# A FoX and RWKV-7 layer: weight sums of seven-part products made ahead, during the input projections, and kept in memory; eight sets a pair instead of six

## The chip, the core and the metric

The kernel runs on one core of a Trainium2 chip. The metric is the device time of one launch in microseconds (us). Matrix products run on TensorE (PE; its weight loads are PEld), two-input vector work on VectorE (DVE), casts and activations on ScalarE (ACT), some element-wise work on GpSimd (POOL). SyncE (SP) issues nearly all DMA transfers.

## What is computed

One layer on 256 rows of width 4096: an input projection, two groups of heads, an output projection, a layer norm. The attention and the recurrence are left out here; they run beside the projections in both kernels.

```python
proj = jnp.einsum('bsd,dc->bsc', x, w_in)           # 256 x 4096 by 4096 x about 16,600
...
h = jnp.concatenate([fox_out, rwkv_out], axis=-1) * jax.nn.silu(z.astype(f32))
out = jnp.einsum('bsc,cd->bsd', h.astype(x.dtype), w_out)   # 256 x 4096 by 4096 x 4096
x = _layernorm(ALPHA * x.astype(f32) + out.astype(f32), ln_gain, ln_bias, LN_EPS).astype(x.dtype)
```

All of it is float32. PE multiplies a rounded type (fp32r) faster than float32, so each operand is cut into a rounded part `hi` and the rest `lo`, and a product is three matmuls: hi by hi, lo by hi, hi by lo.

## The kernel before

**Jobs.** The weights come in jobs of two k-rows of 128 by 512 columns: 128x1024 float32, 512 KB. `load` (L268) has SP fetch one into one of four raw buffers (tag "wr"). `split` makes `hi` by a cast on ACT (L151, four buffers) and `lo` by a subtraction on DVE (L152, three buffers). `fetch` and `weights` keep three jobs made ahead of the one that PE works on; up to three more are loaded or loading. In the input projections a job has 12 matmuls (L157, L158, L159): two k-rows, two halves of 128 rows, three matmuls each. There are 8 groups n of 4 column blocks b of 16 jobs, the first block apart.

**Sides.** The gates, the recurrence (`chain`), the attention and the moving of results are Python generators, each advanced one step at every `slot()`, two slots a job. So their instructions stand between those of the projections, at places that counted waits (`wait(n)`) choose. Each engine takes its instructions in the order in which they were written.

**Output projection.** `plan` lists the jobs of 8 blocks of 512 columns. Blocks 0, 1, 2 and 7 are plain (kind "n"): four `product` calls of three matmuls (L994, L995, L997), so 12 matmuls. Blocks 3 and 4, and 5 and 6, form pairs. For the q in `FEW`, two k-rows of both blocks of a pair are one 2x2 product of blocks, done in a seven-part scheme (Winograd's form of Strassen's): seven products, 21 matmuls, in place of eight products, 24. They are four jobs: e1 (two products with the weights of block b as they are), e2 (one product, half a job of block b+1), e3 and e4 (two products each with sums of weights). The partial results p1, p5, p6, p7 have banks of their own and are added into the output by `merge` when the pair's last set is done. `FEW = range(6, 12)`: six sets a pair, twelve in all.

**Sums.** The left factors (sums of quarters of h) are made by GpSimd in `combine_left` and cut into hi and lo in `split_left`, which writes `sq` and overwrites half of `ht[2q]`; six DMAs restore that half before block 7. The weight sums are made by GpSimd in `combine` (kinds t12: L309, L310; t34: L312, L313), four 128x512 subtractions a set, in the output projection, right before the jobs that use them. To have more raw weights in memory at once, the sets of every second q use places of their own (L259 in tag "lr", L265 in columns of `res`). `drain` runs deferred work (the merges, the residual) at points of the plan.

Of the kernel before, what the change touches and what calls it, by code (L numbers as in the profile page):

```python
# [17 lines left out]
P = 128  # L18
# [72 lines left out]
def layer(ctx: ExitStack, tc: tile.TileContext, xt, xtok, w_main, w_lora, w_first, muv, w_o, up, par, mulora, fbias, lng, lnb, cst, out):  # L91
# [128 lines left out]
    plan += [("n", 2, q) for q in sorted(range(KT // 2), key=lambda q: q not in FEW)]  # L220
    own_place = set()
    for b in (3, 5):
        plain = [[(n, q) for q in range(KT // 2) if q not in FEW] for n in (b, b + 1)]
        units = []
        for q in FEW:
            units.append([plain[j].pop(LEAD if not j else 0) for j in range(2)])
        lead = plain[0]
        assert len(lead) == LEAD
        plan += [("n", *t) for t in lead[: LEAD - 2]]
        for n, q in enumerate(FEW):  # L230
            if n % 2 == 0:
                own_place.add((b, q))
            before = units[n - 1][1] if n else lead[-1]
            plan += [] if n else [("n", *lead[-2])]
            plan += [("t12", b, q), ("n", *before)] + ([("e4", b, FEW[n - 1])] if n else [])
            plan += [("t34", b, q), ("e1", b, q), ("n", *units[n][0]), ("e2", b, q), ("e3", b, q)]
        plan += [("n", *units[-1][1]), ("e4", b, FEW[-1])]
        plan += [("n", *t) for t in plain[1]]
    plan += [("n", NB - 1, q) for q in range(KT // 2)]
    loads = []  # L240
    for kind, b, q in plan:
        loads += [(b, q)] if kind == "n" else [(b, q), (b + 1, q)] if kind == "t12" else []
    stream += [(f"wo{b}_{q}", w_o[b][:, 2 * q : 2 * q + 2, :]) for b, q in loads]
# [7 lines left out]
    sums_of = {}  # L251

    def load():
        name, src = stream.pop()
        b, q = [int(t) for t in name[2:].split("_")] if name[:2] == "wo" else (0, 0)
        if b in PAIRS and (PAIRS[b], q) in own_place:
            if b == PAIRS[b]:
                raw = const.tile([P, 1024], F32, tag="lr", name=name)
                nc.sync.dma_start(out=raw, in_=src.rearrange("p k c -> p (k c)"))  # L259
                apart[name] = [raw[:, j * OB : (j + 1) * OB] for j in range(2)]  # L260
                apart[name, 0] = raw
            else:
                apart[name] = [res[j][:, (NB - 1) * OB :] for j in range(2)]
                for j in range(2):
                    nc.sync.dma_start(out=apart[name][j], in_=src[:, j, :])  # L265
            return
        raw = wpool.tile([P, 1024], F32, tag="wr", name=name, bufs=4)
        nc.sync.dma_start(out=raw, in_=src.rearrange("p k c -> p (k c)"))  # L268
        raws[name] = raw

    def fetch():
        while len(raws) < 3 and stream:
            load()
        job = jobs.pop()
        if job[0][0] in "et":
            combine(*job)
            return
        name = job[0] if len(job) == 1 else f"wo{job[1]}_{job[2]}"
# [12 lines left out]

    apart = {}

    def halves_of(name):
        while name not in raws and name not in apart:
            load()
        if name in apart:
            return apart[name]
        return [raws[name][:, j * OB : (j + 1) * OB] for j in range(2)]

    def combine(kind, b, q):
        one, two = f"wo{b}_{q}", f"wo{b + 1}_{q}"
        if kind in ("t12", "t34", "e2"):
            (b11, b21), (b12, b22) = (halves_of(t) if t == two or kind != "e2" else (None, None) for t in (one, two))
        g = nc.gpsimd.tensor_tensor
        if kind[0] == "t":
            t = sums_of[b, q, kind] = rpool.tile([P, 2 * OB], F32, tag="t", name=f"{kind}_{b}_{q}", bufs=2)
            if kind == "t12":
                g(t[:, :OB], b12, b11, ALU.subtract)  # L309
                g(t[:, OB:], b22, t[:, :OB], ALU.subtract)  # L310
            else:
                g(t[:, :OB], b22, b12, ALU.subtract)  # L312
                g(t[:, OB:], b21, sums_of[b, q, "t12"][:, OB:], ALU.subtract)  # L313
            return
        if kind == "e1":
            t, n = apart.get((one, 0)), 2 * OB
            t = raws.pop(one) if t is None else t
        elif kind == "e2":
            t, n = b22, OB
            raws.pop(two, None)  # L320
        else:
            t, n = sums_of[b, q, "t12" if kind == "e3" else "t34"], 2 * OB
        ready.append(((kind, b, q), *split(t, n, f"{kind}_{b}_{q}")))
# [557 lines left out]

    def chain():
        for n in range(G // 2):
            yield from rwkv(n)
# [131 lines left out]
    def combine_left(q):  # L1016
        e, o = ht[2 * q], ht[2 * q + 1]
        t = lefts[q] = rpool.tile([P, 2 * OB], F32, tag="t", name=f"sf{q}", bufs=2)
        he, ho = t[:, :S], t[:, S : 2 * S]
        s1, s2, s3, s4 = (t[:, 2 * S + n * P : 2 * S + (n + 1) * P] for n in range(4))  # L1020
        g = nc.gpsimd.tensor_tensor
        g(he, e[:, 0, :].bitcast(F32), e[:, 1, :].bitcast(F32), ALU.add)
        g(ho, o[:, 0, :].bitcast(F32), o[:, 1, :].bitcast(F32), ALU.add)
        g(s1, he[:, P:], ho[:, P:], ALU.add)
        g(s2, s1, he[:, :P], ALU.subtract)
        g(s3, he[:, :P], he[:, P:], ALU.subtract)
        g(s4, ho[:, :P], s2, ALU.subtract)

    def split_left(q):
        t = lefts.pop(q)  # L1030
        sq[q] = rpool.tile([P, 2, 3 * P], F32R, tag=f"s{q}", name=f"sq{q}")
        for d, r in ((sq[q], t[:, 2 * S + P :]), (ht[2 * q][:, :, P:], t[:, 2 * S : 2 * S + P])):
            nc.scalar.copy(d[:, 0, :], r)
            nc.vector.tensor_tensor(d[:, 1, :], r, d[:, 0, :].bitcast(F32), ALU.subtract)
        if q + 2 in FEW:
            combine_left(q + 2)
# [4 lines left out]
    def merge(b, kind):  # L1041
# [63 lines left out]
    def halves(b):  # L1105
        o = slice(b * OB, (b + 1) * OB)
        if b == HALVED - 1:
            t = rpool.tile([P, 2 * OB], F32R, tag="t", name=f"g{b}", bufs=2)
            gx[b] = [t[:, :OB], t[:, OB:]]
        else:  # L1110
            gx[b] = [rpool.tile([P, 2, 3 * P], F32R, tag=f"s{FEW[2 * b + j]}", name=f"g{'hl'[j]}{b}").rearrange("p a c -> p (a c)")[:, :OB] for j in range(2)]
# [7 lines left out]
    side(chain())  # L1119
    vt = None  # L1120
# [34 lines left out]
    def banks(b):  # L1155
        if b in oacc:
            return
        if b in (3, 5):
# [27 lines left out]
    def finished(b):  # L1186
# [9 lines left out]
        if b not in (3, 5):  # L1196
# [7 lines left out]
    count = {3: 0, 5: 0}  # L1204
    whole = len(FEW) * 6 + LEAD
    for kind, b, q in plan:
        if kind[0] == "t":
            continue
# [8 lines left out]
        elif b > 1:  # L1217
            drain(2 if b == NB - 1 else q in (0, 1, 3, 5, 13))
        if kind != "n":
# [4 lines left out]
            elif kind == "e2":  # L1224
                product(oacc[b + 1][0], sqof(q, 2), part(hi, 0), part(lo, 0))
# [12 lines left out]
        for j in range(2):  # L1238
# [38 lines left out]
        if (b, q) == (0, KT // 2 - 1):  # L1277
            for i in range(2):
                combine_left(FEW[i])
        if b < NB - 1 and b not in (3, 5) and togo[id(acc[1])][0] == 0:  # L1280
            finished(b)
            if b == 1:
                todo.extend(lambda q=q: split_left(q) for q in FEW)
# [176 lines left out]
```

## Time and profile before

| | us |
|---|---|
| median of 3 runs (lowest, highest) | 1912.85 (1912.48, 1913.59) |
| the profiled execution's own time | 1911.68 |
| its span in the trace | 1909.9 |
| input projections, in the span | to 1536 |
| pairs of the output projection | about 1680 to 1840 |

A busy PE is one that has any matmul in flight: in the timeline a matmul of 512 columns has a length of 0.39 us, but the next one starts 0.23 us after it where nothing holds it up. The granted clock of PE is 1.00 in the whole span. In the views below a group row gives line, engine, operation, output from input, shape and count, then busy us and mean ns of one, then the idle time of the engine before them and what ended it.

### The profile page before, as it was taken

To read this page: it belongs to the slowest core of one execution; us is meant where nothing else is said; L and a number is where in the kernel's file an instruction comes from. 1 tells how busy PE (TensorE), PEld (TensorE's weight loads), DVE (VectorE), ACT (ScalarE), POOL (GpSimd) and SP (SyncE) were. 2 spreads that over 40 slices of the span, in tenths; PEclk is the share of its full clock that TensorE was granted. 3 is DMA by queue.
4 is the path that set the end of the run, shared out by engine and by line. 5 is a ranking of instruction groups with operands and counts; after the bars stand their busy time and mean duration, and the time that the engine had idled before them with its cause. 6 is when DMAs were issued, how large, how long until landed. Compare 5 with 4: busy or idle time off the path is not lost.

```text
span 1909.9 us, 28219 instructions
## 1 busy us (share of the span) xinstructions
PE 1897.6 (99%) x9757; PEld 1575.9 (83%) x9757; DVE 1478.2 (77%) x2417; ACT 1009.2 (53%) x1577; POOL 402.2 (21%) x550
## 2 busy tenths in 40 slices
PE   9999999999999999999999999999999999999998
PEld 9887888888888888888888888888888878877786
DVE  7578768776877687768776877687778775799996
ACT  6554555456545654465546554645464554455453
POOL 0022102210211022002200220022002202386530
PEclk9999999999999999999999999999999999999999
DMA  9678767776777677766876687678767976766665
GB/s 349 181 211 228 207 196 228 231 220 187 232 225 230 188 220 234 226 192 211 241 220 194 207 245 225 192 209 245 217 196 219 306 252 190 236 209 215 203 226 185
DMA packets 272323, 421.37 MB, mean 221 GB/s; under 512 B 142578, under 2 KB 171396, under 8 KB 272180
## 3 DMA queue, kind: packets, MB, share of 16 engines
q1 hardware_dynamic: 271892, 419.23, 72.2%
q8 instruction: 76, 1.25, 0.3%
q14 instruction: 67, 0.55, 0.1%
q10 hardware_dynamic: 288, 0.34, 0.1%
HBM read 389.86 MB, written 29.64 MB: 220 GB/s over the span
## 4 chain that ended last, share of the span: by engine, by line
PE 95%; DVE 2%; POOL 1%; DMA 1%; ACT 0%; issue 0%; SPq 0%; DVEq 0%; ACTq 0%; POOLq 0%
PE acc L157 24%; PE acc L159 24%; PE acc L158 24%; PE oacc L997 5%; PE oacc L994 5%; PE oacc L995 5%; PE rh L740 1%; PE gp L626 1%; PE up L771 1%; PE sp L781 1%; PE accl L159 0%; PE p L997 0%; PE p L995 0%; PE p L994 0%; PE accl L158 0%; PE accl L157 0%
## 5 line engine op out<-in xcount | busy, mean ns | idle before, releaser
L855 POOL COPY pT<-lg 32x96 f32<-32x96 f32 x128 | 55.6, 434 | 630.4 <-DVE lg L851 625.6
L663 POOL COPY BKt<-BK 32x192 f32<-32x192 f32 x128 | 73.5, 574 | 62.8 <-DVE BK L660 57.8
L696 DVE TENSOR_REDUCE xc<-prod 128x8 f32<-128x16 f32 (+30 forms) x248 | 72.7, 293 | 6.6
L693 DVE TENSOR_TENSOR prod<-Nb,xc 128x8 f32<-128x8 f32 (+30 forms) x248 | 72.2, 291 | 3.0
L152 DVE TENSOR_TENSOR w_0l<-w,w_0h 128x1024 fp32r<-128x1024 f32 x31 | 38.2, 1231 | 32.0 <-ACT w_0h L151 23.1
L151 ACT CAST w_0h<-w 128x1024 fp32r<-128x1024 f32 x31 | 32.5, 1048 | 56.8 <-DMA w<-in_w_main_dram 33.1
L151 ACT CAST w_6h<-w 128x1024 fp32r<-128x1024 f32 x31 | 32.7, 1055 | 47.0 <-PE acc L158 36.9
L151 ACT CAST w_8h<-w 128x1024 fp32r<-128x1024 f32 x31 | 32.6, 1053 | 42.5 <-PE acc L158 22.0
L152 DVE TENSOR_TENSOR w_11l<-w,w_11h 128x1024 fp32r<-128x1024 f32 x31 | 37.9, 1223 | 21.9 <-PE acc L159 16.2
L152 DVE TENSOR_TENSOR w_9l<-w,w_9h 128x1024 fp32r<-128x1024 f32 x31 | 38.0, 1226 | 21.5 <-issue 9.6
L152 DVE TENSOR_TENSOR w_15l<-w,w_15h 128x1024 fp32r<-128x1024 f32 x31 | 38.0, 1227 | 20.1 <-issue 17.9
L152 DVE TENSOR_TENSOR w_10l<-w,w_10h 128x1024 fp32r<-128x1024 f32 x31 | 37.9, 1224 | 19.0 <-issue 6.9
L152 DVE TENSOR_TENSOR w_6l<-w,w_6h 128x1024 fp32r<-128x1024 f32 x31 | 38.9, 1255 | 16.1 <-ACT hry L814 10.3
L151 ACT CAST w_10h<-w 128x1024 fp32r<-128x1024 f32 x31 | 32.6, 1053 | 34.4 <-DMA w<-in_w_main_dram 17.9
L157 PE MATMUL acc<-w_15h,x 128*128 128x512 f32 x124 | 50.2, 405 | 0.0
L157 PE MATMUL acc<-w_9h,x 128*128 128x512 f32 x124 | 50.0, 403 | 0.0
L552 POOL COPY hr<-hr 32x16 f32<-32x16 f32 x64 | 44.3, 692 | 26.8 <-DVE hr L549 24.4
L159 PE MATMUL acc<-w_12l,x 128*128 128x512 f32 x124 | 48.5, 391 | 1.1 <-DVE w_12l L152 1.1
L152 DVE TENSOR_TENSOR w_7l<-w,w_7h 128x1024 fp32r<-128x1024 f32 x31 | 37.9, 1222 | 15.1 <-PE acc L159 13.1
L157 PE MATMUL acc<-w_14h,x 128*128 128x512 f32 x124 | 49.5, 399 | 0.0
L151 ACT CAST w_1h<-w 128x1024 fp32r<-128x1024 f32 x31 | 32.7, 1054 | 31.6 <-PE acc L158 15.9
L157 PE MATMUL acc<-w_2h,x 128*128 128x512 f32 x124 | 49.2, 397 | 0.0
(1032 smaller groups left out, 6884.8 us busy)
## 6 DMA issues: line engine op xcount, KB each, us to landing
w<-in_w_main_dram SPq DMA_DIRECT2D x496, 512.0 KB, 4.1
wo<-in_w_o_dram SPq DMA_DIRECT2D x122, 512.0 KB, 4.4
bt<-bk SPq DMA_DIRECT2D x88, 128.0 KB, 3.7
Nb<-nd SPq DMA_DIRECT2D x16, 512.0 KB
hd<-hl SPq DMA_DIRECT2D x29, 256.0 KB
h<-hd SPq DMA_DIRECT2D x29, 256.0 KB, 5.9
wr<-in_w_first_dram SPq DMA_DIRECT2D x15, 384.0 KB, 6.4
lr<-in_w_lora_dram SPq DMA_DIRECT2D x15, 336.0 KB, 6.0
```

The costliest lines, as they stand in the source:

```text
L151: latest[1] = nc.scalar.copy(hi[:, :n], src[:, :n])
L152: latest[0] = nc.vector.tensor_tensor(lo[:, :n], src[:, :n], hi[:, :n].bitcast(F32), ALU.subtract)
L157: nc.tensor.matmul(acc[:, :n], xs[k][:, 0, tt], hi[:, o : o + n], start=(k == 0), stop=False)
L158: nc.tensor.matmul(acc[:, :n], xs[k][:, 1, tt], hi[:, o : o + n], start=False, stop=False)
L159: nc.tensor.matmul(acc[:, :n], xs[k][:, 0, tt], lo[:, o : o + n], start=False, stop=(k == KT - 1))
L663: nc.gpsimd.tensor_copy(BKt[B * b : B * (b + 1), :, :, B * a : B * (a + 1)], BK[B * a : B * (a + 1), :, : NCH - 1, B * b : B * (b + 1)])
L693: first = nc.vector.tensor_tensor(prod[:, :, :, s + 1 :], nb[:, :, s : s + 1, s + 1 :].to_broadcast([P, 2, NJ, w]), xc[:, :, :, s + 1 :], ...
L696: solved = nc.vector.tensor_reduce(xc[:, :, :, s : s + 1], prod[:, :, :, s:], AX.X, ALU.add)
L855: (nc.gpsimd.tensor_copy if b % 2 else nc.scalar.copy)(pT[B * b : B * (b + 1), :, B * a : B * (a + 1)], lg[B * a : B * (a + 1), :, B * b : ...
L994: nc.tensor.matmul(acc, h, hi, start=n[0] == n[1], stop=False)
L995: nc.tensor.matmul(acc, l, hi, start=False, stop=False)
L997: nc.tensor.matmul(acc, h, lo, start=False, stop=not n[0])
```

## The change

- `FEW` has eight values (4 to 11), so sixteen sets in all; a unit of the plan is now e1, e2, one plain job, e3, e4, after four plain jobs, and the remaining four plain jobs follow the eight units.
- A new side, `weight_sums`, runs beside the input projections. For each of the 16 sets it loads the four weight tiles (1 MB), makes four sums on GpSimd and stores the result (1 MB) in DRAM, `tds[b, q]`. One round takes 33 slots of its own waits; the tile `ts` has one buffer.
- e3 and e4 load their weights from `tds` like any other job, e2 loads half a job. All go through the four raw buffers. `combine`, the own places and the six restoring DMAs are gone.
- The left sums move from GpSimd to DVE and are made in block 2, one step (a set's sums, or its split) at each job; they have tiles of their own and no longer overwrite h.
- The order of the additions in `merge` changes with the form of the scheme.

```diff
-FEW = range(6, 12)
+FEW = range(4, 12)
+STARTS = (3, 5)
+REST = 13
...
+    for b in STARTS:
+        plain = [("n", n, q) for n in (b, b + 1) for q in range(KT // 2) if q not in FEW]
+        plan += plain[:LEAD]
         for n, q in enumerate(FEW):
-            if n % 2 == 0:
-                own_place.add((b, q))
...
-            plan += [("t12", b, q), ("n", *before)] + ([("e4", b, FEW[n - 1])] if n else [])
-            plan += [("t34", b, q), ("e1", b, q), ("n", *units[n][0]), ("e2", b, q), ("e3", b, q)]
+            plan += [("e1", b, q), ("e2", b, q), plain[LEAD + n], ("e3", b, q), ("e4", b, q)]
+        plan += plain[LEAD + len(FEW) :]
...
+    tds = {(b, q): dram.tile([P, 4, OB], F32, name=f"td{b}_{q}") for b in STARTS for q in FEW}
+    def source(kind, b, q):
+        two = slice(2 * q, 2 * q + 2)
+        if kind in ("n", "e1"):
+            return w_o[b][:, two, :]
+        if kind == "e2":
+            return w_o[b + 1][:, 2 * q + 1 : 2 * q + 2, :]
+        return tds[b, q][:, 2:4] if kind == "e3" else tds[b, q][:, 0:2]
...
         raw = wpool.tile([P, 1024], F32, tag="wr", name=name, bufs=4)
-        nc.sync.dma_start(out=raw, in_=src.rearrange("p k c -> p (k c)"))
+        nc.sync.dma_start(out=raw[:, : src.shape[1] * OB], in_=src.rearrange("p k c -> p (k c)"))
...
-            ready.append((job, *split(raw, 1024, name)))
+            ready.append((job, *split(raw, OB if job[0] == "e2" else 2 * OB, name)))
...
+    def weight_sums():
+        g = nc.gpsimd.tensor_tensor
+        for b, q in tds:
+            t = rp.tile([P, 4, OB], F32, tag="ts", name=f"ts{b}_{q}")
+            for n in range(2):
+                issue(t[:, 2 * n : 2 * n + 2], w_o[b + n][:, 2 * q : 2 * q + 2, :])
+            yield from wait(6)
+            b11, b21, b12, b22 = (t[:, n] for n in range(4))
+            for o, x, y in ((b11, b12, b11), (b12, b22, b12), (b22, b22, b11), (b21, b21, b22)):
+                g(o, x, y, ALU.subtract)
+                yield from wait(2)
+            yield from wait(REST)
+            issue(tds[b, q], t)
+            yield from wait(6)
...
     def combine_left(q):
-        g = nc.gpsimd.tensor_tensor
+        g = nc.vector.tensor_tensor
...
     def split_left(q):
-        sq[q] = rpool.tile([P, 2, 3 * P], F32R, tag=f"s{q}", name=f"sq{q}")
-        for d, r in ((sq[q], t[:, 2 * S + P :]), (ht[2 * q][:, :, P:], t[:, 2 * S : 2 * S + P])):
-            nc.scalar.copy(d[:, 0, :], r)
-            nc.vector.tensor_tensor(d[:, 1, :], r, d[:, 0, :].bitcast(F32), ALU.subtract)
-        if q + 2 in FEW:
-            combine_left(q + 2)
+        r = lefts.pop(q)[:, 2 * S :]
+        d = sq[q] = rpool.tile([P, 2, 4 * P], F32R, tag=f"s{q}", name=f"sq{q}")
+        nc.scalar.copy(d[:, 0, :], r)
+        nc.vector.tensor_tensor(d[:, 1, :], r, d[:, 0, :].bitcast(F32), ALU.subtract)
...
+    side(weight_sums())
...
-            drain(2 if b == NB - 1 else q in (0, 1, 3, 5, 13))
+            drain(2 if b == NB - 1 else 1)
...
             elif kind == "e3":
-                product(p5, rowsof(2 * q, 1), part(hi, 0), part(lo, 0))
-                product(p6, sqof(q, 0), part(hi, 1), part(lo, 1))
+                product(p7, sqof(q, 2), part(hi, 0), part(lo, 0))
+                product(p6, sqof(q, 1), part(hi, 1), part(lo, 1))
             else:
-                product(p7, sqof(q, 1), part(hi, 0), part(lo, 0))
+                product(p5, sqof(q, 0), part(hi, 0), part(lo, 0))
...
-                todo.extend(lambda q=q: split_left(q) for q in FEW)
+                todo.extend(lambda f=f, q=q: f(q) for q in FEW for f in (combine_left, split_left))
```

What this does to the order on the engines is shown at three places. Rows give the line, the operation, and output from input with its shape; names end in a running number.

The first is SP's queue in the first pair, around set q = 8. `wo3_8` is the job of block 3 and q = 8; in the kernel before:

```order
L268 DMA wo4_0_16359<-in_w_o_dram 128x1024
L259 DMA wo3_8_16428<-in_w_o_dram 128x1024
L268 DMA wo3_5_16397<-in_w_o_dram 128x1024
L971 DMA lg5_16988<-in_lng_dram 128x512
L265 DMA res1_15799<-in_w_o_dram 128x512
L268 DMA wo4_1_16432<-in_w_o_dram 128x1024
L268 DMA wo3_12_16444<-in_w_o_dram 128x1024
L268 DMA wo3_9_16456<-in_w_o_dram 128x1024
L268 DMA wo4_9_16484<-in_w_o_dram 128x1024
```

In the changed kernel `e33_8` is kind e3, block 3, q = 8, and `td3_8` is its place in DRAM:

```order
L255 DMA e13_8_16716<-in_w_o_dram 128x1024
L255 DMA e23_8_16725<-in_w_o_dram 128x512
L255 DMA wo4_0_16743<-in_w_o_dram 128x1024
L255 DMA e33_8_16755<-td3_8_844 128x1024
L255 DMA e43_8_16767<-td3_8_844 128x1024
L255 DMA e13_9_16779<-in_w_o_dram 128x1024
L255 DMA e23_9_16788<-in_w_o_dram 128x512
```

A set had four loads, two of them of plain jobs and some in places of their own; a unit has five, one of a plain job, one of half size, all through the raw buffers.

The second is DVE at the same place: the subtractions that make `lo`. Before, from `e4` of q = 7:

```order
L152 TENSOR_TENSOR e4_3_7l_16487<-t34_3_7_16409,e4_3_7h_16486 128x1024
L152 TENSOR_TENSOR e1_3_8l_16512<-wo3_8_16428,e1_3_8h_16511 128x1024
L152 TENSOR_TENSOR wo3_12l_16528<-wo3_12_16444,wo3_12h_16527 128x1024
L152 TENSOR_TENSOR e2_3_8l_16540<-res1_15799,e2_3_8h_16539 128x512
L152 TENSOR_TENSOR e3_3_8l_16550<-t12_3_8_16474,e3_3_8h_16549 128x1024
L152 TENSOR_TENSOR wo4_2l_16569<-wo4_2_16537,wo4_2h_16568 128x1024
```

And in the changed kernel:

```order
L154 TENSOR_TENSOR e13_8l_16746<-e13_8_16716,e13_8h_16745 128x1024
L154 TENSOR_TENSOR e23_8l_16758<-e23_8_16725,e23_8h_16757 128x512
L154 TENSOR_TENSOR wo4_0l_16770<-wo4_0_16743,wo4_0h_16769 128x1024
L154 TENSOR_TENSOR e33_8l_16782<-e33_8_16755,e33_8h_16781 128x1024
L154 TENSOR_TENSOR e43_8l_16791<-e43_8_16767,e43_8h_16790 128x1024
```

The inputs of e3 and e4 were tiles that GpSimd wrote (`t12`, `t34`); now they are loaded buffers. A set has six subtractions before (two of plain jobs) and a unit five.

The third is POOL in the input projections, in the second group of the recurrence (`chain`). Before:

```order
L552 COPY hr2_3010<-hr2_3010 32x16 x4
L836 AFFINE_SELECT nb2_3734<-nb2_3734 128x128 x2
L630 TENSOR_TENSOR vs1_3137<-vs1_3137,bk1_1_3133 128x512
L631 TENSOR_TENSOR vs1_3137<-vs1_3137,muv1_2646 128x512
L632 TENSOR_TENSOR vs1_3137<-vs1_3137,bk1_1_3133 128x512
L552 COPY hr3_3210<-hr3_3210 32x16 x4
L532 MEMSET eL4_4791 128x4
L628 TENSOR_TENSOR BK1_2988<-BK1_2988,lc1_2987 128x2x384
```

And in the changed kernel, where `ts3_9` holds the weights of block 3, q = 9:

```order
L503 COPY hr3_3266<-hr3_3266 32x16 x4
L483 MEMSET eL4_4876 128x4
L581 TENSOR_TENSOR vs1_3193<-vs1_3193,bk1_1_3189 128x512
L582 TENSOR_TENSOR vs1_3193<-vs1_3193,muv1_2694 128x512
L583 TENSOR_TENSOR vs1_3193<-vs1_3193,bk1_1_3189 128x512
L842 TENSOR_TENSOR ts3_9_3296<-ts3_9_3296 128x512 x4
L579 TENSOR_TENSOR BK1_3043<-BK1_3043,lc1_3042 128x2x384
L614 COPY BKt1_3514<-BK1_3043 32x6x32 x16
```

The four sums of a set stand in one piece among the recurrence's own work.

More of the change, by code (lines that the diff above doesn't have):

```diff
@@ L219, in layer @@
     plan = [("n", b, q) for r in (range(CUT), range(CUT, KT // 2)) for b in range(2) for q in r]
[L220 to L229, printed above, removed]
-        for n, q in enumerate(FEW):
-            if n % 2 == 0:
-                own_place.add((b, q))
-            before = units[n - 1][1] if n else lead[-1]
-            plan += [] if n else [("n", *lead[-2])]
-            plan += [("t12", b, q), ("n", *before)] + ([("e4", b, FEW[n - 1])] if n else [])
-            plan += [("t34", b, q), ("e1", b, q), ("n", *units[n][0]), ("e2", b, q), ("e3", b, q)]
-        plan += [("n", *units[-1][1]), ("e4", b, FEW[-1])]
-        plan += [("n", *t) for t in plain[1]]
@@ L239, in layer @@
-    plan += [("n", NB - 1, q) for q in range(KT // 2)]
[L240 to L243, printed above, removed]
+    plan += [("n", 2, q) for q in range(KT // 2)]
+    for b in STARTS:
+        plain = [("n", n, q) for n in (b, b + 1) for q in range(KT // 2) if q not in FEW]
+        plan += plain[:LEAD]
+        for n, q in enumerate(FEW):
+            plan += [("e1", b, q), ("e2", b, q), plain[LEAD + n], ("e3", b, q), ("e4", b, q)]
+        plan += plain[LEAD + len(FEW) :]
@@ L244, in layer @@
+    stream += [(named(*t), source(*t)) for t in plan]
     jobs = [(f"w{n}_{b}_{q}",) for n in range(G // 2) for b in range(4) for q in range(KT // 2) if n or b] + plan
@@ L250, in layer @@
     raws = {}
-    sums_of = {}
     def load():
         name, src = stream.pop()
[L255 to L258, printed above, removed]
-                nc.sync.dma_start(out=raw, in_=src.rearrange("p k c -> p (k c)"))
[L260 to L266, printed above, removed]
         raw = wpool.tile([P, 1024], F32, tag="wr", name=name, bufs=4)
-        nc.sync.dma_start(out=raw, in_=src.rearrange("p k c -> p (k c)"))
+        nc.sync.dma_start(out=raw[:, : src.shape[1] * OB], in_=src.rearrange("p k c -> p (k c)"))
         raws[name] = raw
@@ L274, in fetch @@
         job = jobs.pop()
[L275 to L278, printed above, removed]
+        name = job[0] if len(job) == 1 else named(*job)
         raw = raws.pop(name)
         if name not in kept:
-            ready.append((job, *split(raw, 1024, name)))
+            ready.append((job, *split(raw, OB if job[0] == "e2" else 2 * OB, name)))
             return
@@ L290, in fetch @@
         ready.append((job, hl[:2], hl[2:]))
[L292 to L304, printed above, removed]
-        g = nc.gpsimd.tensor_tensor
[L306 to L323, printed above, removed]
     def weights(job):
@@ L1106, in halves @@
         o = slice(b * OB, (b + 1) * OB)
[L1107 to L1111, printed above, removed]
+        t = rpool.tile([P, 2, OB], F32R, tag=f"s{FEW[b]}", name=f"g{b}")
+        gx[b] = [t[:, 0], t[:, 1]]
         with tc.issue_after(latest[0].ins), tc.issue_after(latest[1].ins):
@@ L1157, in banks @@
             return
-        if b in (3, 5):
+        if b in STARTS:
             few = len(FEW)
@@ L1195, in finished @@
                 (behind if step is not add else todo).append(lambda step=step, m=m: step(m, b))
-        if b not in (3, 5):
+        if b not in STARTS:
             todo.extend(behind)
@@ L1202, in layer @@
     behind = []
-    count = {3: 0, 5: 0}
-    whole = len(FEW) * 6 + LEAD
+    count = dict.fromkeys(STARTS, 0)
+    whole = len(FEW) * 5 + LEAD
     for kind, b, q in plan:
-        if kind[0] == "t":
-            continue
         banks(PAIRS.get(b, b))
@@ L1224, in layer @@
             elif kind == "e2":
[L1225 removed]
+                product(oacc[b + 1][0], sqof(q, 3), part(hi, 0), part(lo, 0))
             elif kind == "e3":
[L1227 to L1228 removed]
+                product(p7, sqof(q, 2), part(hi, 0), part(lo, 0))
+                product(p6, sqof(q, 1), part(hi, 1), part(lo, 1))
             else:
[L1230 removed]
+                product(p5, sqof(q, 0), part(hi, 0), part(lo, 0))
                 product(oacc[b][1], rowsof(2 * q + 1, 1), part(hi, 1), part(lo, 1))
@@ L1276, in layer @@
             nc.vector.memset(lneps, LN_EPS)
[L1277 to L1280, printed above, removed]
+        if b < NB - 1 and b not in STARTS and togo[id(acc[1])][0] == 0:
             finished(b)
             if b == 1:
-                todo.extend(lambda q=q: split_left(q) for q in FEW)
+                todo.extend(lambda f=f, q=q: f(q) for q in FEW for f in (combine_left, split_left))
             elif b == 6:
```

15 lines of the change are left out of this document (6 added, 9 removed).

## The prediction

> **What bounds the kernel now.** The head of the page comes first.
>
> ```profile
> span 1909.9 us, 28219 instructions
> PE 1897.6 (99%) x9757; PEld 1575.9 (83%) x9757; DVE 1478.2 (77%) x2417; ACT 1009.2 (53%) x1577; POOL 402.2 (21%) x550
> ```
>
> PE is busy for all but 12 us of the span, so only two things shorten the program: fewer matmuls, or fewer places where PE waits. The table by stretches says where it waits. Its columns are the stretch in us, its length, then the busy time (and count) of PE, PEld, DVE, ACT and POOL, PE's granted clock, the DMA share and GB/s.
>
> ```profile
> 264.00:453.00 189.00, 189.00 (x999) 157.24 (x998) 145.04 (x257) 101.27 (x163) 30.87 (x54) 1.00 0.74 218
> 1402.00:1550.00 148.00, 148.00 (x748) 123.12 (x748) 116.73 (x209) 79.67 (x129) 27.16 (x49) 1.00 0.80 253
> 1660.00:1850.00 190.00, 187.36 (x809) 150.47 (x809) 177.26 (x145) 98.11 (x109) 125.33 (x69) 1.00 0.62 206
> 1760.00:1780.00 20.00, 20.00 (x90) 16.53 (x90) 18.20 (x23) 8.01 (x8) 4.54 (x2) 1.00 0.82 265
> 1780.00:1800.00 20.00, 19.23 (x84) 15.44 (x83) 18.12 (x13) 10.25 (x11) 14.09 (x8) 1.00 0.56 183
> ```
>
> In the two first stretches, of the input projections (the second reaches into the first jobs after them), PE never rests, and DVE still has 44 of 189 us free. In the stretch with the seven-part products, 1660 to 1850, PE rests 2.64 us, DVE is busy for 177 of 190 us and POOL for 125. Within it PE is whole where POOL is quiet (1760 to 1780) and not where POOL works (1780 to 1800). The timeline of PE shows the first and the last of 13 such places (start, duration, instruction, idle time and releaser).
>
> ```profile
> 1676.59 0.39 PE L994 MATMUL oacc<-wo_15h,hl 128*128 128x512 f32 x1
> 1676.82 0.39 PE L995 MATMUL oacc<-wo_15h,hl 128*128 128x512 f32 x1
> 1677.75 0.50 PE L997 MATMUL oacc<-wo_15l,hl 128*128 128x512 f32 x1 [0.55 <-DVE wo_15l L152]
> 1678.09 0.40 PE L994 MATMUL oacc<-wo_15h,hl 128*128 128x512 f32 x1
> ...
> 1832.26 0.39 PE L995 MATMUL oacc<-wo_15h,hl 128*128 128x512 f32 x1
> 1832.74 0.50 PE L997 MATMUL oacc<-wo_15l,hl 128*128 128x512 f32 x1
> 1833.08 0.40 PE L994 MATMUL oacc<-wo_15h,hl 128*128 128x512 f32 x1
> ```
>
> Undisturbed matmuls start 0.23 us apart (1676.59 to 1676.82). From 1676.82 to 1678.09 two steps take 1.27 where 0.46 would do: 0.81 lost. At 1832.26 it is 0.82 - 0.46 = 0.36. Each time the third matmul, with the lo half, waits for DVE's L152. The timeline of DVE and POOL says why DVE is late.
>
> ```profile
> 1710.43 2.32 DVE L152 TENSOR_TENSOR e_8l<-wo,e_8h 128x1024 fp32r<-128x1024 f32 x1
> 1711.63 2.28 POOL L312 TENSOR_TENSOR t<-res,res 128x512 f32<-128x512 f32 x1
> 1712.67 2.32 DVE L152 TENSOR_TENSOR wo_12l<-wo,wo_12h 128x1024 fp32r<-128x1024 f32 x1
> 1713.88 2.27 POOL L313 TENSOR_TENSOR t<-wo,t 128x512 f32<-128x512 f32 x1
> 1717.76 1.21 DVE L152 TENSOR_TENSOR wo_2l<-wo,wo_2h 128x1024 fp32r<-128x1024 f32 x1
> ```
>
> Beside a POOL sum the subtraction takes 2.32 us, without one 1.21: each two-input instruction of the one engine holds up the other's, by 1.1 us for DVE.
>
> **The change, part by part.** My base is the profiled execution, 1911.68 us, of which 1909.9 are the span and the rest lies around it; the median, 1912.85, is 1.2 above it.
>
> (1) Fewer products. A seven-part set has 7 products in place of 8, each of three matmuls, so a set saves 3. There are 16 sets where there were 12: 4 x 3 = 12 matmuls x 0.23 = **-2.8 us**. PE is full there, so all of it counts.
>
> (2) No POOL sums beside the output projection. The 48 weight sums and the left sums leave POOL in this stage. PE's 13 late places are 2.64 us of idle time in the window's row, and each hides some 0.2 more under the longer records beside it (0.39 and 0.50 where the step is 0.23); summed by starts, as in the two places above, they are 5.4 us. What would be late next is DVE itself, but its L152 instructions fall from 2.32 to 1.21. I take **-5.4 us**; the ends are 0, if part (4) makes DVE as late, and -5.4.
>
> (3) Weights in the sets. Before, a set was spread over about 10 us with two plain jobs; now one unit is e1, e2, one plain job, e3, e4, and DVE does only its five subtractions: 7 products and the plain job's 4 are 33 matmuls x 0.23 = 7.6 us on PE. It takes five loads through the four buffers of tag "wr", and a buffer is free only when its weights have landed and both halves are made. Rows for these steps, as groups (line, names, count | busy, mean ns | idle before), and the landing of loads (median us):
>
> ```profile
> wo<-in_w_o_dram SPq DMA_DIRECT2D x96, 512.0 KB, 4.4
> DMA to landing us min/median/max: 3.4/4.5/6.4
> L151 ACT CAST wo_1h<-wo 128x1024 fp32r<-128x1024 f32 x4 | 4.2, 1053 | 3.8 <-PE oacc L995 3.8
> L152 DVE TENSOR_TENSOR w_7l<-w,w_7h 128x1024 fp32r<-128x1024 f32 x31 | 37.9, 1222 | 15.1 <-PE acc L159 13.1
> L152 DVE TENSOR_TENSOR e_6l<-res,e_6h 128x512 fp32r<-128x512 f32 x2 | 1.4, 684 | 0.3 <-PE oacc L997 0.3
> ```
>
> With landing L, a full load holds its buffer L + 1.05 + 1.22 = L + 2.3 us; e2, half as wide, about 1 us less. Five holds over four buffers take (5L + 10.4) / 4 = 1.25 L + 2.6 us a unit. At L = 3.4 that is 6.9, under PE's 7.6; at 4.4 it is 8.1, **0.5 late**; at 5 it is 8.9, 1.3 late; the rings agree at L = 4.0. The first three units of each pair live on buffers filled during the plain jobs, so 5 units x 2 pairs x 0.5 = 5. DMA has to move 4.5 x 524 KB in 7.6 us, 310 GB/s, beyond any row above (265 at a share of 0.82). I take the median landing, **+5 us**; the ends are 0 (L = 3.4) and 7 units x 2 x 1.3 = 18 (L = 5).
>
> The Trainium skill's page "SBUF — State Buffer", section "The DMA setup-cost knee", speaks against this price: it gives a transfer about 2 us of fixed cost and then 436 GB/s, by which 512 KB would land in 3.2 us (an estimate from that page), and the ring would never starve. The trace's median of 4.4 disagrees, and its minimum of 3.4 is near; how often loads come near the minimum in a dense unit, no run shows so far.
>
> (4) The weight sums beside the input projections. They are 16 units of 4 sums, 64 in all, in blocks (0,1) to (4,1), some 770 us; in a unit the four stand together in POOL's order, behind one landing. DVE runs two-input instructions there for most of its time.
>
> ```profile
> 314.36 1.52 DVE L589 TENSOR_TENSOR lt<-s,eL 128x256 f32<-128x256 f32 x1
> 317.11 1.36 POOL L632 TENSOR_TENSOR vs<-vs,bk 128x512 f32<-128x512 f32 x1
> 318.78 1.22 DVE L152 TENSOR_TENSOR w_5l<-w,w_5h 128x1024 fp32r<-128x1024 f32 x1
> 320.28 0.39 PE L159 MATMUL acc<-w_5l,x 128*128 128x512 f32 x1
> DVE w_3l L152 <- PE acc L159: 14.5, 15, 1.5
> L474 DVE TENSOR_TENSOR hl<-h,hl 128x256 fp32r<-128x256 f32 x32 | 13.4, 420 | 3.8 <-ACT hl L473 3.8
> ```
>
> POOL's sums here already stretch DVE: L589 takes 1.52 us at 314.36 beside one, while an op of its size, L474, has a mean of 0.42. At most 64 x 1.1 = 70 us of stretching meets 770 x 44/189 = 179 us of free DVE time, so on the whole it fits: the waits of DVE show that it often stands until PE frees a lo buffer (15 times for w_3l), which means that it runs ahead. The cover is that lead. It is not everywhere: w_5l ends at 320.00 and PE takes it at 320.28, 0.28 us later. A unit of four sums in such a place costs 4 x 1.1 less the lead, some 3 to 4 us; most units fall where DVE is several us ahead. I take one such place, **+3.5 us**; the ends are 0 and four places, 4 x 3.5 = 14.
>
> What the unit queues: its store stands in SP's queue until the sums are done, and the weight loads stand behind it, so a late POOL would stall them. It is issued 13 slots (of 1.36 us) after the last sum, against 4 x 1.36 of work; I cost it at nothing, covered by the three jobs made ahead and the loaded buffers. On POOL, the chain's copies stand behind the sums, and those wait for a load that was issued 6 slots (8 us) before. The 33.6 MB of traffic are 44 GB/s over 770 us: 218 + 44 = 262, close to the 253 that the 148-us row carries with PE whole; nothing. In the sets only loads are left: the six loads that restored h go, as do the own-place loads.
>
> (5) Left sums on VectorE, during block 2 at one step per job: for a set, two sums of 128x256 (0.42, L474) and four of 128x128, then a 128x512 subtraction.
>
> ```profile
> 1653.98 0.28 DVE L1034 TENSOR_TENSOR h<-sf,h 128x128 fp32r<-128x128 f32 x1
> ```
>
> Together 2 x 0.42 + 4 x 0.28 + 0.68 = 2.6 us per two jobs, plus their 2 x 1.22: 5.1 of the 24 x 0.23 = 5.5 us that PE needs. It hides, barely; nothing, and up to +3 where PSUM evictions of block 1 come beside it. Lead built up earlier covers some of that.
>
> **Sum** against the profile: -2.8 - 5.4 + 5 + 3.5 = +0.3, 1912.0; on the median's scale **1913.2 us**. I take 0.2%, 3.8 us (about what a measurement of this kernel can tell from no change), as the bound: 1909.0 to 1916.7.
>
> **Rivals.**
> A: both costs hide. The loads come alone on DMA now in the output stage, their landing stays near 3.4 to 4.0, and the sums fall into DVE's free time. For it: PE is whole at 265 GB/s, and 179 us are free. Against it: median 4.4. It leaves 1 us of costs: 1912.85 - 8.2 + 1 = 1905.7.
> B, slower: the four buffers starve PE in the units. At 310 GB/s loads land in 5 us or more; then 14 units x 1.3 = 18 in place of 5: 1913.2 + 13 = 1926. It decides from L = 4.5 (0.6 x 14 = 8.4, which eats the gain). For it: the landing's maximum of 6.4 and a rate that no row carries; against it, a starved ring asks for less at once and so lands sooner.
> C, slower: the POOL sums of the input phase find DVE without lead in four units, not one: 1913.2 + 10.5 = 1923.7. For it: 0.28 us of lead at 320; against it, DVE's long waits for PE elsewhere.
> That the change does nothing is excluded by the order of instructions: twelve matmuls and all of POOL's sums leave the output projection. A store read too early cannot cost anything either; some 800 us lie between.
>
> **How the numbers follow.** The forecast has 0.34 (own range 1908 to 1918), A 0.31, B 0.19, C 0.16. The range takes in A to its full gain (1912.85 - 8.2 = 1904.6), C, and B's lower half: 1904 to 1925, which leaves out under 2 in 10. Faster: A and 0.04 of the forecast, 0.35. Same: 0.28 of the forecast. Slower: B, C and 0.02, 0.37.
>
> **What would show it.** (1) Twelve matmuls fewer than the 9757 of the page. (2) L152's successor never takes 2.3 us after 1660, and PE's places before lo matmuls are gone. (3) PE's waits in the units name DMA or ACT's cast behind a load, from the fourth unit on, some 0.5 us a unit; starts of e1 8 us apart, not 7.6. (4) Around each group of four sums on POOL, DVE subtractions of 2.3 us, and in one or two of 16 units a PE idle time behind L154 between 70 and 840 us. (5) PE whole in block 2. I am wrong at the root if PE loses over 5 us between 70 and 840, or if the units keep to 7.6 us with landings of 4.4 and more.

## The result, and the profile after

| | us |
|---|---|
| median of 4 runs of the changed kernel (lowest, highest) | 1957.85 (1953.23, 1963.30) |
| the kernel before, beside them | 1912.83 (1912.48, 1913.59) |
| ratio | 1.0236 (95% interval 1.0207 to 1.0265) |
| the profiled execution's own time; its span | 1960.14; 1958.4 |

The change costs 45 us, where the prediction had 0.3 and a range that ended at 12. Where they come from is read by comparing the start of the same job in both traces (the first matmul of a block's first job), which gives three parts of the 48.5 us between the two spans: 25.4 up to the last block of the input projections, 21.5 more up to block 7 of the output projection (the pairs), 1.6 behind. (In the kernel before, block 7 starts at 1852.2, so the pairs fill 1680 to 1852 us.) Of the 25.4, 25.1 are there by 900 us, when the last of the 16 sets has been stored; from 946 us to the end of the input projections the difference doesn't change by 0.1.

The head of the page, and the table by stretches of the changed kernel (columns as before); the last line is the kernel before in the stretch with the weight sums.

```profile
span 1958.4 us, 28349 instructions
PE 1915.0 (98%) x9745; PEld 1574.4 (80%) x9745; DVE 1484.7 (76%) x2469; ACT 1012.2 (52%) x1581; POOL 361.9 (18%) x530
```

```profile
60.00:860.00 800.00, 783.73 (x4083) 643.75 (x4081) 621.90 (x1039) 409.73 (x666) 228.64 (x289) 1.00 0.80 249
1402.00:1550.00 148.00, 148.00 (x760) 123.29 (x759) 111.45 (x201) 81.94 (x142) 29.03 (x53) 1.00 0.76 236
1715.00:1795.00 80.00, 69.87 (x279) 51.56 (x278) 47.97 (x46) 40.05 (x43) 0.00 (x0) 0.98 0.75 251
```

```profile
60.00:860.00 800.00, 798.78 (x4192) 663.45 (x4191) 606.92 (x1068) 430.33 (x692) 130.39 (x231) 1.00 0.73 215
```

PE has twelve matmuls fewer, as the change says. It now rests 16 us of the first 800 (1 before), and 10 of the 80 us of the first pair's units. Where no sums are made (1402 to 1550) it is whole. In the units DVE is busy for 60% of the time, ACT for half and POOL not at all: nothing there is short of an engine.

**In the units** PE waits for casts and for the subtractions behind them. First its waits between 1700 and 1900 (engine, line, waited for: us, times, longest), then the timeline of ACT, DVE and SP's queue over one unit.

```profile
PE p L960 <- ACT e_11h L153: 3.2, 2, 2.3
PE p L960 <- ACT e_10h L153: 2.4, 3, 1.1
PE p L960 <- ACT e_7h L153: 1.6, 2, 1.0
PE p L963 <- DVE e_10l L154: 1.6, 3, 0.5
```

```profile
1739.69 1.23 DVE L154 TENSOR_TENSOR e_6l<-e,e_6h 128x1024 fp32r<-128x1024 f32 x1 [2.07 <-ACT e_6h L153]
1740.94 1.57 SPq L255 DMA_DIRECT2D e<-td  x2
1742.78 1.82 SPq L255 DMA_DIRECT2D e<-in_w_o_dram  x2
1744.89 1.05 ACT L153 CAST e_7h<-e 128x1024 fp32r<-128x1024 f32 x1 [1.91 <-DMA e<-td]
1745.97 1.23 DVE L154 TENSOR_TENSOR e_7l<-e,e_7h 128x1024 fp32r<-128x1024 f32 x1 [1.74 <-ACT e_7h L153]
1747.23 0.33 SPq L255 DMA_DIRECT2D wo<-in_w_o_dram  x1
1747.95 1.05 ACT L153 CAST e_7h<-e 128x1024 fp32r<-128x1024 f32 x1 [2.01 <-DMA e<-td]
1749.21 1.57 ACT L153 CAST e_8h<-e 128x1024 fp32r<-128x1024 f32 x2 [0.22 <-DMA e<-in_w_o_dram]
```

This is the ring at work. A subtraction ends at 1740.92, and 0.02 us later SP issues the load that takes its buffer (e3 of q = 7). Its cast, which waits for nothing but that load, starts at 1744.89: 3.95 us. Its subtraction ends at 1747.20, and at 1747.23 the next load goes out. The three loads issued at 1742.2, 1742.8 and 1744.3 land one behind the other: e4 is cast at 1747.95, 5.8 us after its issue, e1 at 1749.21, 6.4 us after. From the third unit on, the starts of e1 in the first pair are 9.7 us apart on average ((1780.47 - 1732.01) / 5), and 9.7 in the second ((1878.70 - 1829.99) / 5). Over the 25 loads that go out in the first pair from e3 of q = 6 on (1730.95 to 1775.15), a buffer is held for 7.7 us on average from the issue to the end of the subtraction, and five holds over four buffers are 5 x 7.7 / 4 = 9.6 us a unit: the ring accounts for the whole step.

**In the input projections** the sums do what they did in the output projection. This is the timeline of POOL and DVE, and the matmul behind them, in block (2,1), which loses most:

```profile
478.78 5.02 POOL L842 TENSOR_TENSOR ts<-ts 128x512 f32<-128x512 f32 x3
479.70 1.52 DVE L770 TENSOR_TENSOR post<-post 128x256 f32<-128x256 f32 x1
481.25 1.40 DVE L771 TENSOR_TENSOR post<-post,bon 128x256 f32<-128x256 f32 x1
482.57 2.30 DVE L154 TENSOR_TENSOR w_8l<-w,w_8h 128x1024 fp32r<-128x1024 f32 x1
```

```profile
484.93 0.50 PE L161 MATMUL acc<-w_8l,x 128*128 128x512 f32 x1 [1.42 <-DVE w_8l L154]
```

Three DVE instructions in a row each take about 1.1 us more than without a sum beside them (0.42 and 1.22), and PE waits 1.42 us for the third. The Trainium skill's page "SBUF — State Buffer", section "SBUF: two separate sides", states that GpSimd and a VectorE instruction with two SBUF inputs lock a pair of ports against each other for a whole instruction; the 2.30 us here agree with that.

### The profile page after: what moved, and what is told of

It reads as the page before. It is cut to its first block, busy times and chain, and to the rows that moved or that the text cites. A ratio compares the mean times of both kernels' runs of the same rounds, so it can differ in the third digit from the quotient of the medians.

```text
span 1958.4 us, 28349 instructions
## 1 busy us (share of the span) xinstructions
PE 1915.0 (98%) x9745; PEld 1574.4 (80%) x9745; DVE 1484.7 (76%) x2469; ACT 1012.2 (52%) x1581; POOL 361.9 (18%) x530
## 4 chain that ended last, share of the span: by engine, by line
PE 81%; DVE 7%; DMA 7%; ACT 2%; SPq 1%; issue 1%; DVEq 0%; ACTq 0%; POOL 0%
PE acc L161 21%; PE acc L159 21%; PE acc L160 20%; PE oacc L963 4%; PE oacc L960 4%; PE oacc L961 4%; DMA e<-td 2%; DMA w<-in_w_main_dram 2%; DMA e<-in_w_o_dram 1%; SPq L318 1%; PE rh L691 1%; PE gp L577 1%; DVE prod L644 1%; PE up L722 1%; PE sp L732 1%
## 5 line engine op out<-in xcount | busy, mean ns | idle before, releaser
L842 POOL TENSOR_TENSOR ts<-ts 128x512 f32<-128x512 f32 x64 | 100.4, 1568 | 182.9 <-DMA ts<-in_w_o_dram 177.6
L644 DVE TENSOR_TENSOR prod<-Nb,xc 128x8 f32<-128x8 f32 (+30 forms) x248 | 78.1, 315 | 2.9
L154 DVE TENSOR_TENSOR w_0l<-w,w_0h 128x1024 fp32r<-128x1024 f32 x31 | 37.9, 1222 | 36.5 <-ACT w_0h L153 25.4
L154 DVE TENSOR_TENSOR w_11l<-w,w_11h 128x1024 fp32r<-128x1024 f32 x31 | 39.8, 1284 | 21.9 <-ACT w_11h L153 11.6
L154 DVE TENSOR_TENSOR w_7l<-w,w_7h 128x1024 fp32r<-128x1024 f32 x31 | 40.4, 1305 | 19.3 <-ACT w_7h L153 8.6
L154 DVE TENSOR_TENSOR w_10l<-w,w_10h 128x1024 fp32r<-128x1024 f32 x31 | 38.8, 1251 | 20.3 <-ACT w_10h L153 12.2
L503 POOL COPY hr<-hr 32x16 f32<-32x16 f32 x64 | 38.4, 600 | 78.6 <-DVE hr L500 76.2
L161 PE MATMUL acc<-w_11l,x 128*128 128x512 f32 x124 | 47.6, 397 | 4.1 <-DVE w_11l L154 4.1
L154 DVE TENSOR_TENSOR w_8l<-w,w_8h 128x1024 fp32r<-128x1024 f32 x31 | 40.8, 1317 | 14.3 <-ACT w_8h L153 10.5
L787 POOL TENSOR_SCALAR_AFFINE_SELECT nb<-nb 128x128 f32<-128x128 f32 x32 | 22.7, 716 | 153.5 <-DMA nb<-ncd 93.5
L154 DVE TENSOR_TENSOR w_6l<-w,w_6h 128x1024 fp32r<-128x1024 f32 x31 | 38.9, 1254 | 15.6 <-PE acc L161 7.5
L159 PE MATMUL acc<-w_10h,x 128*128 128x512 f32 x124 | 49.6, 400 | 1.0 <-ACT w_10h L153 1.0
L154 DVE TENSOR_TENSOR w_15l<-w,w_15h 128x1024 fp32r<-128x1024 f32 x31 | 38.5, 1242 | 15.3 <-issue 13.1
```

Source lines behind the costliest of these rows:

```text
L154: latest[0] = nc.vector.tensor_tensor(lo[:, :n], src[:, :n], hi[:, :n].bitcast(F32), ALU.subtract)
L159: nc.tensor.matmul(acc[:, :n], xs[k][:, 0, tt], hi[:, o : o + n], start=(k == 0), stop=False)
L161: nc.tensor.matmul(acc[:, :n], xs[k][:, 0, tt], lo[:, o : o + n], start=False, stop=(k == KT - 1))
L644: first = nc.vector.tensor_tensor(prod[:, :, :, s + 1 :], nb[:, :, s : s + 1, s + 1 :].to_broadcast([P, 2, NJ, w]), xc[:, :, :, s + 1 :], ...
L842: g(o, x, y, ALU.subtract)
```

## The experiments

The theories at this point: the pairs lose to the ring of four raw buffers (R), against a DMA that can't carry more (M) or stored sums that land late; the input stage loses to POOL's sums (P), against their transfers (D). In the edits "..." stands for lines left as they were. "Input", "pairs" and "behind" in the tables are differences to the kernel before in the profiled executions, as above; the changed kernel has 25.4, 21.5, 1.6. Each is read from one execution; the four runs of the changed kernel lie within 10 us of each other, and those of the kernels with four raw buffers within 3 to 9.

**No sums.** The side `weight_sums` is left out.

```diff
-        return tds[b, q][:, 2:4] if kind == "e3" else tds[b, q][:, 0:2]
+        return w_o[b + 1][:, two, :] if kind == "e3" else w_o[b][:, two, :]
...
-    side(weight_sums())
```

> The changed kernel without its side that makes the weight sums; e3 and e4 load plain weights of the same size from w_o, so that the output is not the layer's. The output projection keeps all its instructions. If the loss up to 840 us (25.4 us in the trace) comes from the side and the loss behind it (23 us) from the ring of raw buffers, this takes 1957.9 - 25 = 1932 us, and the units of the pairs still start 9 to 10 us apart. A rival says that loads from the stored sums land later than loads from w_o: then the pairs, too, come near 7.6 us a unit, and the time falls to about 1905.

1926.11 us, ratio 1.0059 (1.0042 to 1.0077); input 0.9, pairs 15.5, behind 1.1. The input loss is the side's, all of it, and the pairs stay slow with plain weights. So stored sums are not what makes the units slow, though the pairs lose 6 us less here than in the changed kernel; what those are is taken up below.

**POOL alone.** The 64 sums on one tile of zeros, without loads and stores; e3 and e4 load plain weights as above.

```diff
-        for b, q in tds:
-            t = rp.tile([P, 4, OB], F32, tag="ts", name=f"ts{b}_{q}")
-            for n in range(2):
-                issue(t[:, 2 * n : 2 * n + 2], w_o[b + n][:, 2 * q : 2 * q + 2, :])
+        t = rp.tile([P, 4, OB], F32, tag="ts", name="ts")
+        nc.gpsimd.memset(t, 0.0)
+        for _ in range(2 * len(FEW)):
...
-            issue(tds[b, q], t)
```

> The 64 sums on POOL at the same slots, but on one tile of zeros, without the loads and without the stores; e3 and e4 load plain weights. Theory P (the sums hold up DVE's two-input instructions, rival C of the prediction) expects most of the 25 us here: about 1950 to 1957. Theory D (the loads and stores of the sums make the projections' weights land later) expects no loss before 840 us: about 1932 to 1936.

1981.82 us, ratio 1.0362 (1.0346 to 1.0377): slower than the changed kernel. The trace says why it was no fair test: input 56.0, nearly all of it before 210 us.

```profile
60.00:210.00 150.00, 105.76 (x456) 85.21 (x454) 116.53 (x106) 48.90 (x72) 119.90 (x89) 0.84 0.45 129
```

With nothing to wait for, POOL made its sums in one run at the start, busy for 120 of these 150 us. The counted slots set an order on an engine, not a time; only a dependency does. What it does show is that back to back the sums cost far more, 56 / 64 = 0.9 us each. Some of that is PE's own clock, which fell to 0.84 in this row (last section).

**Transfers alone.** Loads and stores stay, the subtractions go (their waits stay), so that e3 and e4 get plain weights from the stored copies.

```diff
-            for o, x, y in ((b11, b12, b11), (b12, b22, b12), (b22, b22, b11), (b21, b21, b22)):
-                g(o, x, y, ALU.subtract)
-                yield from wait(2)
+            yield from wait(8)
```

> The loads and stores of the side at the same slots, without the 64 sums on POOL, so that e3 and e4 get plain weights from the stored copies. Theory P expects about 1932 to 1936, theory D 1950 to 1958. If each is needed for the other (a late weight leaves DVE no lead, and then a sum costs), e2 and e3 together lose clearly less than the 25 us.

1937.16 us, ratio 1.0132 (1.0113 to 1.0152); input 6.4, pairs 16.2, behind 1.1. The transfers alone cost 5.5 us more than no side at all (0.9). That is nearer to theory P, but it isn't nothing. It is a lower end, too: the profiled execution (1935.33) is the fastest of this kernel's four, and the medians of the two kernels are 11 us apart.

**POOL alone, paced.** As "POOL alone", but each set is held back by four loads of 8 KB.

```diff
+            for n in range(4):
+                issue(t[:, n, :16], w_o[0][:, n, :16])
             yield from wait(6)
```

> The 64 sums on POOL without the large loads and the stores, but each set held back by four small loads (8 KB each) issued where the changed kernel issues its 1 MB; e3 and e4 load plain weights. The input stage lost 25 us with sums and transfers and 6 us with transfers alone. If the sums cost by themselves what is left, this loses about 19 us before 860 us in the trace and takes 1926 + 19 = 1945 us. If a sum only hurts where a late weight has used up DVE's lead, it loses under 8 us: below 1934.

1942.41 us, ratio 1.0153 (1.0136 to 1.0170); input 17.3, pairs 12.0, behind 1.7. The 16.4 us above "no sums" are the price of the sums, with the 64 small loads that pace them and one stretch of slow clock (1.6 us, last section). The stretches of this kernel and of "no sums":

```profile
60.00:860.00 800.00, 788.99 (x4116) 649.00 (x4115) 632.27 (x1046) 416.71 (x673) 233.69 (x296) 1.00 0.72 211
```

```profile
60.00:860.00 800.00, 798.37 (x4187) 662.34 (x4186) 606.10 (x1066) 428.85 (x691) 130.50 (x231) 1.00 0.73 214
```

DVE is busy 26 us longer for fewer instructions, and some 170 us of its time stay free; 16.4 us of delay reach PE all the same.

**Five raw buffers.** Paid for with one buffer of `lg`; `fetch` keeps four loads ahead instead of three.

```diff
-        raw = wpool.tile([P, 1024], F32, tag="wr", name=name, bufs=4)
+        raw = wpool.tile([P, 1024], F32, tag="wr", name=name, bufs=5)
...
-        while len(raws) < 3 and stream:
+        while len(raws) < 4 and stream:
...
-        lgain[b] = rpool.tile([P, OB], F32, tag="lg", name=f"lg{b}", bufs=3)
+        lgain[b] = rpool.tile([P, OB], F32, tag="lg", name=f"lg{b}", bufs=2)
```

> The changed kernel with five raw buffers instead of four and four loads ahead instead of three, paid for with one buffer of lg less. The output is the layer's. The ring theory: five holds of L + 2.3 us over five buffers are 7.6 us at L = 5.5, so the 30 us lost in the units shrink to 0 to 10; with the input stage unchanged 1930 to 1940, and if a fifth buffer also covers late landings there, 1910 to 1930. The rival, that DMA itself can't carry 310 GB/s in the units, expects landings to grow with the fifth buffer and the units to stay at 9 to 10 us: 1950 to 1958.

1927.60 us, ratio 1.0078 (1.0063 to 1.0093); input 17.7, pairs -5.5, behind 1.3. The pairs went from a loss of 21.5 to a gain of 5.5. Most units of the first pair start 7.6 us apart, PE's own pace. In the two stretches below, five buffers stand first and the changed kernel second:

```profile
1700.00:1880.00 180.00, 178.03 (x773) 144.48 (x772) 141.97 (x151) 101.15 (x109) 0.00 (x0) 1.00 0.87 292
```

```profile
1700.00:1880.00 180.00, 164.43 (x669) 124.64 (x669) 120.95 (x131) 88.26 (x95) 0.00 (x0) 0.98 0.76 249
```

DMA moved 292 GB/s there, so M falls: 249 was what the ring asked for, not what DMA could do. The input loss fell as well, from 25.4 to 17.7, with POOL's sums unchanged.

**Sums on VectorE.** DVE makes the 64 sums, 12 slots behind their loads.

```diff
-        g = nc.gpsimd.tensor_tensor
+        g = nc.vector.tensor_tensor
...
-            yield from wait(6)
+            yield from wait(12)
...
-            yield from wait(REST)
+            yield from wait(REST - 6)
```

> The changed kernel with the 64 sums on VectorE, 12 slots behind their loads instead of 6 (and the store as much nearer). A sum takes DVE about 0.68 us there, 44 us in all, where a collision with POOL costs up to 1.1, 70 us in all. If the hold of the one engine by the other is what the sums cost, the input stage loses about 6 us for the transfers and 0 to 6 for DVE: 1938 to 1944 us in place of 1958. If any extra work for DVE there costs as much, it stays at 1950 to 1958.

1947.93 us, ratio 1.0183 (1.0165 to 1.0200); input 13.4, pairs 21.1, behind 0.3. The input loss is halved, which fits neither end of what was expected: 44 us of extra work for DVE still cost 7 above the transfers.

**Both cures.** Five raw buffers and the sums on VectorE.

> Both cures together: five raw buffers and the sums on VectorE. If the two losses are separate, the input stage loses 3 to 10 us and the output projection gains about 4 (as with five buffers alone): 1912 to 1919 us. If the fifth buffer also takes up the late landings, the input stage loses under 4: 1907 to 1912.

1913.50 us, ratio 1.0003 (0.9993 to 1.0012); input 5.7, pairs -5.6, behind 0.8. The fifth buffer also took the input loss from 13.4 to 5.7. Of that, 4.6 lie in blocks (1,0), (2,0) and (4,0), next to none in the blocks between.

**Sums outside the blocks with b = 0**, on top of both cures.

```diff
+    now = [1]
+
...
         for b, q in tds:
+            while not now[0]:
+                yield
...
-            yield from wait(REST - 6)
+            yield from wait(REST - 7)
...
+            now[0] = b
             acc = block(n, b)
```

> Five raw buffers and the sums on VectorE as before, but no set begins in a block with b = 0, so that three sets fall into each group of four blocks. In the trace of that kernel 5.7 us are lost up to 860 us, 4.6 of them in blocks (1,0), (2,0) and (4,0). If the place in the group is what counts, 1 to 2 us remain: 1913.5 - 4 = 1909 to 1910 us. If the sets only push each other's loss to another block, it stays at 1912 to 1914.

1910.84 us, ratio 0.9992 (0.9983 to 1.0000); input 3.7, pairs -5.8, behind 0.3. Blocks (2,0) and (4,0) lose 0.2 at most now; 2.0 are left in block (1,0).

**From the second group on**, on top of that: `now[0] = b * n` and `now = [0]` at first, so that the first set begins in block (1,1).

> As the kernel that skips the blocks with b = 0, but the sets begin in block (1,1) instead of (0,1). Of the 3.7 us that the other one's trace loses up to 860 us, 2.0 are in block (1,0). If that is the recurrence's first group, which is late only beside the sets' transfers, about 2 us go: 1909 us, faster than before by 0.2%. If the first sets lose them wherever they begin, it stays at 1911.

1909.38 us, ratio 0.9982 (0.9973 to 0.9991); input 2.1, pairs -3.5, behind 0.3. This is the only kernel with the layer's output that is clear of the one before. Block (1,0) loses nothing; of the pairs' gain, 1.6 us went in this profile in one stretch of slow clock (last section).

**Five buffers, no sums**: what the new output projection is worth alone.

> Five raw buffers and no weight sums at all; e3 and e4 load plain weights, so that the output is not the layer's. It shows what the new output projection is worth alone once the ring is eased. The kernel with both cures gained 4.8 us behind 860 us in the trace, so 1912.8 - 4.8 = 1908 us is expected, and at the least 1904.6 (the full 8.2 us of the prediction's terms 1 and 2). If the stored sums land later than plain weights and cost something in the units, it is nearer 1905.

1903.98 us, ratio 0.9954 (0.9940 to 0.9968); input 0.7, pairs -7.8, behind 0.3. It is the last of the expected cases. The three kernels with five buffers and stored sums whose profiles are free of a stretch of slow clock in the pairs have -5.5, -5.6 and -5.8 there. So loads of stored sums seem to cost the pairs about 2 us more than loads of plain weights; with four buffers the values scatter too widely to say it (stored 21.5, 16.2 and 21.1, plain 15.5, 16.4 and 12.0). Why, no run shows.

## Why the prediction was wrong

**Terms (1) and (2), the gain of 8.2 us, were right in sum.** With the ring eased and no sums the pairs gain 7.8 us, and the median falls by 8.6. The two weren't measured apart.

**Term (3), the ring, had the right mechanism and the wrong size.** The prediction put it as "I take the median landing, **+5 us**", with L = 4.4, the median of a kernel that asked for 206 GB/s in its pairs: 14 of its 46 raw-buffer loads from 1690 to 1840 us went out while no other of them was under way, where none of the changed kernel's 83 from 1725 to 1890 did. In the units three loads go out within 2 us and land one behind the other, cast 4.0, 5.8 and 6.4 us after their issue as shown. Turned round, its own formula gives L = 5.7 from the 9.7 us a unit, outside its upper end of L = 5. Most of that is the landing (5.5 us from issue to cast, on average over the 25 loads); the rest is e2, which the formula made 1 us cheaper than a full load and which holds its buffer for 8.1 us, since it lands behind e1 and its cast and subtraction queue behind e1's. The ring's cost is the pairs with four buffers against five: 21.5 + 5.5 = 27 us, where 5 stood and 18 was the end. "A starved ring asks for less at once and so lands sooner" was the argument against rival B, and it was wrong in itself: loads go out close together, because buffers come free close together. The estimate of 3.2 us from the Trainium skill's page "SBUF — State Buffer", section "The DMA setup-cost knee", holds for none of these three loads, the nearest being the 3.95 us of the first.

**Term (4), the sums beside the input projections, had the right mechanism for the sums, far too small, and nothing for the transfers.** It took "one such place, **+3.5 us**" of 16, on the ground that DVE has 179 us free and is mostly ahead. Between 60 and 850 us PE waits 11 times behind DVE's L154, 11.3 us in all (before: once, 1.1), and 24 us are lost between 70 and 840, where the prediction had called a loss of over 5 wrong at the root. Measured by themselves, the sums cost 16.4 us and the transfers at least 5.5, where "nothing" stood. The rest of the 24.5 above no side (25.4 - 0.9) is 2.6; 1.5 of it is a stretch of slow clock that the changed kernel has more there (two, against one in "POOL alone, paced"; last section), and 1.1 stays open. Two things failed. Free time on average is not free time when it is needed: the loss is largest in single blocks (5.5 us in (2,1) and 4.1 in (2,3), each with a stretch of slow clock in it), while some others lose next to nothing. And the traffic was judged by GB/s, which DMA carried with ease; what it cost was lead, since five buffers instead of four cut the input loss with sums on DVE from 13.4 to 5.7 us.

**The rivals B and C were given as alternatives, and both held.** B was to give 1926, C 1924, each with the other's cost left small. They lie in different stages and need nothing from each other, so their costs add. In the profiled executions -7.8 is the gain of the pairs, 29.3 what they lose of it (21.5 + 7.8, against five buffers and no sums) and 24.5 the price of the side: 46.0. With 0.9 in the input stage that is not the side's and 1.6 behind the pairs that is the 48.5 between the spans. A case in which both hold would have stood at about 1937 by the prediction's own upper prices, and the range should have reached there; the sizes took it beyond.

**Term (5) held.** In block 2, where DVE makes the left sums, the time from the block's job q = 0 to that of the next block is 43.7 us in the changed kernel, and 43.5 in those with five buffers, where 16 jobs of twelve matmuls at 0.227 us need 43.6. The store in SP's queue was costed at nothing; no run tells it from the loads, since both are in the 5.5 us, and "transfers alone" has no sums for the store to wait for. There SP's queue stands still five times, 9.2 us in all, until a store has landed and the next set may be loaded. What the 1.6 us behind the pairs are (0.3 in four of the other kernels) stays open.

## What to carry to other kernels

Price a ring of buffers at the rate its stage will ask for, in the pattern in which its slots come free, not with the landing measured at a lower rate; and where the price hangs on it, one more buffer is the cheapest experiment. Idle time of an engine that feeds the bound one hides nothing by its mean: what counts is its lead at each place, and work put beside it belongs where that lead is longest (here, outside the blocks with b = 0), on the engine that holds up no other. Costs in different stages are not rival cases; they add, and so must the ends of the range.

## What the hardware showed besides

A wait of PE can cost more than its length. After two waits of 1.03 and 0.53 us, the changed kernel's timeline of PE shows eight matmuls with a step of 0.43 us instead of 0.23:

```profile
1846.55 0.50 PE L960 MATMUL p<-e_7h,sq 128*128 128x512 f32 x1 [1.03 <-ACT e_7h L153]
1846.89 0.39 PE L961 MATMUL p<-e_7h,sq 128*128 128x512 f32 x1
1847.81 0.50 PE L963 MATMUL p<-e_7l,sq 128*128 128x512 f32 x1 [0.53 <-DVE e_7l L154]
1848.15 0.45 PE L960 MATMUL oacc<-e_7h,h 128*128 128x512 f32 x1
1848.40 0.63 PE L961 MATMUL oacc<-e_7h,h 128*128 128x512 f32 x1
1848.83 0.63 PE L963 MATMUL oacc<-e_7l,h 128*128 128x512 f32 x1
...
1851.39 0.57 PE L963 MATMUL oacc<-e_8l,h 128*128 128x512 f32 x1
1851.80 0.40 PE L960 MATMUL oacc<-e_8h,sq 128*128 128x512 f32 x1
```

```profile
1844.00:1854.00 10.00, 8.44 (x29) 5.98 (x28) 5.45 (x6) 4.71 (x5) 0.00 (x0) 0.83 0.71 230
```

The granted clock falls to 0.83 over these ten us. From 1848.40 to 1851.80 the array runs at about half its rate, 3.4 us long, and 1.6 us are lost on top of the waits. The changed kernel has four such stretches (at 493.6, 592.3, 1791.1 and 1848.4), together 5.8 us; the kernel before has none. The Trainium skill's page "TensorE: Matmul & The Clock Gate", section "Part 1: The HAM clock gate", states that the clock is halved after an idle window of about 3.4 us and is full again after one of work. The step of 0.43 and the length of 3.4 us agree; but PE was not idle that long before any of the four, and waits of 1.03 and 0.53 us within one such length were enough.

The traces record the stretches themselves. In each trace they begin whole multiples of 3.41 us apart (in the changed kernel the records begin at 493.3, 592.2, 1790.3 and 1848.3), and each lasts 3.41 us or a multiple of it. Cut all twelve traces into such cells, from 60 us to 12 us before the end, and count each matmul as 0.23 us at most: in the cell before each of the 27 slow ones PE worked for 45% of the time or less, and of the 6501 cells before one at full clock only four are as low. So what a wait costs depends on how much else is lost in the same 3.41 us.
